# Delta rule: a chunk's decay is made one chunk ahead of its keys and queries

## The chip, the cores and the metric

The kernel runs on one core of one Trainium2 chip. The metric is device time in microseconds (us) of one execution, the median of several runs. The engines are named as in the profile: PE (TensorE matmuls; PEld its weight loads), DVE (VectorE), ACT (ScalarE), POOL (GpSimd) and SP (SyncE, which issues the DMAs; its queue is SPq).

## The reference, cut to what matters

One layer of a diffusion backbone over 2048 latent tokens and 256 context tokens, with two parallel branches. The change lies in the first one, a gated delta rule with 4 heads, run forwards and backwards. For each head and chunk of tokens it needs the decay between every two tokens of the chunk, from the running sum `G` of the log gates `g`:

```python
G = jnp.cumsum(g, axis=-1)
diff = G[..., :, None] - G[..., None, :]
decay = jnp.where(incl, jnp.exp(jnp.where(incl, diff, 0.0)), 0.0)
a_mat = jnp.where(strict, jnp.einsum('bhncd,bhnsd->bhncs', kb, k) * decay, 0.0)
...                                  # solve with (a_mat + eye)
attn = jnp.einsum('bhncd,bhnsd->bhncs', q, k) * decay
```

So the decay multiplies two products: keys with keys (for the triangular system) and keys with queries (for the attention inside a chunk). It depends on the gates alone, not on keys or queries.

## The kernel before, in words

The kernel works in chunks of 128 tokens: 18 chunks, of which 2 are context. It has these stages, in the order of the code: input norm and projection weights, the projections that give keys, queries and values (stored to DRAM as `qkvD`) and the log gates (`gD`, at about 166 us), the second branch (until about 1050 us), the chunk preparation of the delta rule (`prep`, `solve`, `levels`), the delta rule's steps (`stepA`), and the output stage.

`prep(pos)` (L732 to L806) handles one chunk. `pos` counts through `seq`: both context chunks, then the latent chunks alternately from the front and the back. In it:

- L737/L739 load keys, queries and values of the chunk into `l`, which has one buffer. PE transposes keys (`pk`, L746), queries (`pq`, L753) and values (`pv`, L764); ACT sums the squares of keys (L748) and queries (L755) and copies the transposed keys into `kv` (L749); DVE scales the values into `kv` (L765), for which it needs the norms `sk` (L756, L758) and a power that POOL takes (L757). L766 stores `kv`.
- The decay is made for each direction `d`: L773 loads the row of log gates, broadcast over the partitions, into `gb` (tag `gm`, two buffers); L777 on DVE scans it into `dc` (tag `dec`, two buffers), with a mask (`after`) that starts the sum anew at the diagonal; L779 on ACT takes the exponential; L781 on POOL zeroes the other triangle.
- L785 makes keys by keys (`pkk`), and L788 on DVE multiplies it with the decay into `an`, eight times. For latent chunks L793 makes keys by queries (`pkq`), L795 on DVE multiplies it into the decay tile in place, and L796 stores that tile to DRAM (`atN`). Blocks of `an` then go through `pk_` (L799, L801) and `dg` (L804, L805) to DRAM.

The PSUM tiles `pk`, `pq`, `pv`, `pkk` and `pkq` share one tag (`t`) with three buffers.

`solve` (L808) inverts the 32x32 diagonal blocks of four chunks at a time in a chain of small DVE operations (L821, L823). `levels` (L828) builds the larger inverse from them with small matmuls into `lvt`. In the code four `prep` calls come first, then four `levels` of the group before, then a `solve`.

After this stage the code has the gate projections (`gate_block`, L217, with the matmuls L210 to L212, weights loaded by L200 and split by L201 on ACT and L202 on POOL, results copied by L223 or L225 and stored by L226). They depend on nothing in the preparation.

The order in which each engine takes its instructions is not that of the code. When the program is built, a planner goes through it with its own estimates of durations and gives an engine that is free the earliest instruction in the code that it takes to be ready. This is how gate matmuls come between the matmuls of `prep`, and how operations of a chunk come ahead of others that stand before them in the code. The queues are fixed by then: on the chip each engine takes its instructions strictly in that order, and one that waits holds up those behind it. Buffers of a tag are given out in turn, and a write to one waits until its former content has been read.

Of the kernel before, what the change touches and what calls it, by code (L numbers as in the profile page):

```python
# [8 lines left out]
F32 = mybir.dt.float32  # L9
F32R = mybir.dt.float32r  # L10
U8 = mybir.dt.uint8
AF = mybir.ActivationFunctionType
ALU = mybir.AluOpType
# [3 lines left out]
P = 128  # L17
# [7 lines left out]
H = 4  # L25
NC = TOK // P
# [13 lines left out]
def block_kernel(ctx, tc, x, c, ctx_in, c_ctx, w_mod, b_mod, w_in, conv_w, a_log, dt_bias,  # L40
                 lb_param, a_norm_g, b_norm_g, w_a_out, w_b_out, w_out, ln_g, ln_b, out, dbg=None):
    nc = tc.nc
    sy, te, ve, ac, po = nc.sync, nc.tensor, nc.vector, nc.scalar, nc.gpsimd
# [102 lines left out]
    gD = dr.tile([2, NC, H, P], F32, name="gD")  # L146
# [342 lines left out]
    with tc.tile_pool(name="rb", reuse_waits="tile", bufs=1, side="right") as rb, \  # L489
# [12 lines left out]
        def bl(a):  # L502
            return slice(32 * a, 32 * a + 32)
# [176 lines left out]
        def gate_units(i):  # L680
            w = load_w(gcol[i])
            for g in range(NG):
                yield gate_block(i, [g], w=w)
# [3 lines left out]
        for h in range(H):  # L687
            fill = head_units(h + 1) if h + 1 < H else gate_units(NEARLY + GA)
# [24 lines left out]
    seq = list(range(NCC))  # L713
    for i in range((NC - NCC) // 2):
        seq += [NCC + i, NC - 1 - i]
    with tc.tile_pool(name="rc", reuse_waits="tile", bufs=2, side="right") as rc, \
# [7 lines left out]
        after = [rc.tile([P, H * P], U8, name=f"after{d}", bufs=1) for d in range(2)]  # L724
        for d in range(2):
            po.tensor_copy(out=after[d].rearrange("p (h t) -> p h t", h=H),
                           in_=(m_lt, m_gt)[d].bitcast(F32).unsqueeze(1).to_broadcast([P, H, P]))

        def bl(a):
            return slice(32 * a, 32 * a + 32)  # L730

        def prep(pos):  # L732
            ch = seq[pos]
            lat = ch >= NCC
            l = rc.tile([P, 3, H, P], F32, tag="l", name="l", bufs=1)
            if lat:
                sy.dma_start(out=l, in_=qkvD[ch])  # L737
            else:
                sy.dma_start(out=l[:, 0:3:2], in_=qkvD[ch, :, 0:3:2])  # L739
            kT, qT, vT = l[:, 0], l[:, 1], l[:, 2]  # L740
            kv = rc.tile([P, 2, H, P], F32, tag="kv", name="kv", bufs=1)
            sk = rc.tile([P, H], F32, tag="sk", name="sk")
            nk = rc.tile([P, H], F32, tag="nk", name="nk")
            pt = pc.tile([P, H, P], F32, tag="t", name="pk", bufs=3)
            for h in range(H):
                te.transpose(pt[:, h, :], kT[:, h, :], ident)  # L746
            for h in range(H):
                ac.activation(out=junk, in_=pt[:, h, :], func=AF.Square, accum_out=sk[:, h:h + 1])  # L748
            ac.copy(out=kv[:, 0], in_=pt)  # L749
            if lat:  # L750
                pq = pc.tile([P, H, P], F32, tag="t", name="pq", bufs=3)
                for h in range(H):
                    te.transpose(pq[:, h, :], qT[:, h, :], ident)  # L753
                for h in range(H):
                    ac.activation(out=junk, in_=pq[:, h, :], func=AF.Square, accum_out=sq[:, ch, h:h + 1])  # L755
            ve.tensor_scalar(out=sk, in0=sk, scalar1=EPS, scalar2=None, op0=ALU.add)  # L756
            po.tensor_tensor(out=nk, in0=sk, in1=half.to_broadcast([P, H]), op=ALU.pow)  # L757
            ve.reciprocal(out=sk, in_=sk)  # L758
            ve.scalar_tensor_tensor(out=nbz[:, :, ch, :], in0=beta[:, :, ch, :], scalar=-1.0,
                                    in1=sk.unsqueeze(1).to_broadcast([P, 2, H]), op0=ALU.mult, op1=ALU.mult)  # L760
            ve.tensor_tensor(out=nbze[:, :, ch, :], in0=nbz[:, :, ch, :], in1=erem[:, :, ch, :], op=ALU.mult)
            pv = pc.tile([P, H, P], F32, tag="t", name="pv", bufs=3)
            for h in range(H):
                te.transpose(pv[:, h, :], vT[:, h, :], ident)  # L764
            ve.tensor_tensor(out=kv[:, 1], in0=pv, in1=nk.unsqueeze(2).to_broadcast([P, H, P]), op=ALU.mult)  # L765
            sy.dma_start(out=knvD[ch], in_=kv)  # L766
            an = rc.tile([P, 2, H, P], F32, tag="an", name="an", bufs=1)
            dg = rc.tile([P, 2, H, 32], F32, tag="dg", name="dg", bufs=1)
            dec = []
            for d in range(2):  # L770

                gb = rc.tile([P, H * P], F32, tag="gm", name="gb")
                sy.dma_start(out=gb, in_=gD[d, ch].rearrange("h t -> (h t)").partition_broadcast(P))  # L773
                dc = rc.tile([P, H, P], F32, tag="dec", name="dec")
                dec.append(dc)
                rev = slice(None, None, -1 if d else 1)
                ve.tensor_tensor_scan(out=dc.rearrange("p h t -> p (h t)")[:, rev], data0=gb[:, rev], data1=after[d][:, rev],  # L777
                                      initial=0.0, op0=ALU.add, op1=ALU.mult)
                ac.activation(out=dc, in_=dc, func=AF.Exp)  # L779
                sgn = 1 if d == 0 else -1  # L780
                po.affine_select(out=dc, in_=dc, pattern=[[0, H], [sgn, P]], compare_op=ALU.is_ge, fill=0.0,  # L781
                                 base=0, channel_multiplier=-sgn)
            pkk = pc.tile([P, H, P], F32, tag="t", name="pkk", bufs=3)
            for h in range(H):
                te.matmul(out=pkk[:, h, :], lhsT=kT[:, h, :], rhs=kT[:, h, :], start=True, stop=True)  # L785
            for d in range(2):
                for h in range(H):
                    ve.scalar_tensor_tensor(out=an[:, d, h, :], in0=pkk[:, h, :], scalar=nbz[:, d, ch, h:h + 1],  # L788
                                            in1=dec[d][:, h, :], op0=ALU.mult, op1=ALU.mult)
            if lat:  # L790
                pkq = pc.tile([P, H, P], F32, tag="t", name="pkq", bufs=3)
                for h in range(H):
                    te.matmul(out=pkq[:, h, :], lhsT=kT[:, h, :], rhs=qT[:, h, :], start=True, stop=True)  # L793
                for d in range(2):
                    ve.tensor_tensor(out=dec[d], in0=pkq, in1=dec[d], op=ALU.mult)  # L795
                    sy.dma_start(out=atN[ch, :, d, 0], in_=dec[d])  # L796
            pk_ = rc.tile([P, H, 96], F32, tag="pk", name="pk_", bufs=1)
            for b in range(4):
                ac.copy(out=pk_[bl(b), :, 0:32], in_=an[bl(b), b % 2, :, bl(b ^ 1)])  # L799
            for d in range(2):  # L800
                ve.tensor_copy(out=pk_[64 * d:64 * d + 64, :, 32:96], in_=an[64 * d:64 * d + 64, d, :, 64 - 64 * d:128 - 64 * d])  # L801
            sy.dma_start(out=anD[ch], in_=pk_)
            for b in range(4):
                ve.transpose(out=dg[bl(b), 0].rearrange("p h j -> p (h j)"), in_=an[bl(b), 0, :, bl(b)])  # L804
                ac.copy(out=dg[bl(b), 1], in_=an[bl(b), 1, :, bl(b)])  # L805
            sy.dma_start(out=dgD[pos].rearrange("d h b i j -> (b i) (d h) j"), in_=dg.rearrange("p d h j -> p (d h) j"))  # L806

        def solve(c0, cn):  # L808

            NP = 32 * cn  # L810
            A = rc.tile([P, 32, 32], F32, tag="sA", name="sA", bufs=1)
            X = rc.tile([P, 32, 32], F32, tag="sX", name="sX", bufs=1)
            T = rc.tile([P, 256], F32, tag="sT", name="sT", bufs=1)
            Af, Xf = (t.rearrange("p i j -> p (i j)") for t in (A, X))
            sy.dma_start(out=Af[0:NP], in_=dgD[c0:c0 + cn].rearrange("c d h b i j -> (c d h b) (i j)"))
            po.memset(Xf, 0.0)
            po.memset(Xf[:, 0:1024:33], 1.0)
            for j in range(31):
                m = 31 - j
                t3 = T[0:NP, 0:m * (j + 1)].rearrange("p (i c) -> p i c", c=j + 1)  # L820
                ve.tensor_tensor(out=t3, in0=A[0:NP, j + 1:, j:j + 1].to_broadcast([NP, m, j + 1]),  # L821
                                 in1=X[0:NP, j:j + 1, 0:j + 1].to_broadcast([NP, m, j + 1]), op=ALU.mult)
                ve.tensor_tensor(out=X[0:NP, j + 1:, 0:j + 1], in0=X[0:NP, j + 1:, 0:j + 1], in1=t3, op=ALU.add)  # L823
            ac.copy(out=A[0:NP], in_=X[0:NP].rearrange("p a b -> p b a"))
            for t, i in ((Xf, 0), (Af, 1)):
                sy.dma_start(out=nD[i][c0:c0 + cn].rearrange("c d h b i j -> (c d h b) (i j)"), in_=t[0:NP])
# [93 lines left out]
    if True:  # L920
        SA = []
        for d in range(2):
            t = rd.tile([P, H, P], F32, tag=f"S{d}", name=f"S{d}")
# [78 lines left out]
        for s in range(NC):  # L1002
# [5 lines left out]
            for d in range(2):  # L1008
                ch = order[d][s]
# [205 lines left out]
```

## Time and profile before

| what | value |
|---|---|
| median of 3 runs | 2260.94 us (2259.52 to 2265.21) |
| profiled execution | 2257.96 us, its span 2256.2 us |
| mean granted PE clock | 0.981 |
| PE / DVE / ACT / POOL busy | 95% / 63% / 41% / 30% of the span |
| HBM read and written | 226.27 MB and 110.87 MB |

How to read the profile: an entry of a group gives the line of the kernel, the engine, the operation, output and inputs by name, the count, the busy time and the mean in ns of one. A wait is written as "engine tile line <- who released it: us in total, times, longest us". A wait for several things is put down to the last one. In the table by stretches each engine has its busy us and its number of instructions; the granted clock of PE is a share of full speed. PE idle is the length of a stretch less PE's busy time. Matmul records are modelled at their ends, so busy PE need not be PE at its peak.

### The profile page before, as it was taken

The numbers are of one execution on the slowest core, as the hardware profiler recorded it, in microseconds if no ns is written. First come the engines' busy times: TensorE is split into PE (matmuls) and PEld (weight loads), VectorE is DVE, ScalarE is ACT, GpSimd is POOL, SyncE is SP. The second block draws the span as 40 slices with busy tenths as digits, with TensorE's granted clock in tenths as the row PEclk, the third lists the DMA queues.
The fourth block names the chain that finished last, engine by engine and source line by source line (L and its number), as shares of the span: only waits on it lengthen the run. The fifth ranks groups of instructions, "written<-read, shape, count | busy, mean of one in ns | idle before, by whom it ended". The sixth has DMA issues, their size and how long they took to land. (4 is left out here: it accounts for less than half of the span.)

```text
span 2256.2 us, 40291 instructions
## 1 busy us (share of the span) xinstructions
PE 2135.6 (95%) x15184; PEld 1785.3 (79%) x15184; DVE 1410.5 (63%) x3235; ACT 915.4 (41%) x2314; POOL 670.5 (30%) x666
## 2 busy tenths in 40 slices
PE   7899999999999999999998898999989888999998
PEld 2778888888888888888777677778778877988887
DVE  5927666727776777785588887723332338766664
ACT  3523222224343443442555554343544345444431
POOL 2703434312221222223333332221133224433331
PEclk8999999999999999999999999999999999999999
DMA  8312222322222322225768887867888764444422
GB/s 322 96 57 66 75 65 68 84 82 79 86 83 77 111 74 87 87 72 164 234 220 241 243 241 198 251 199 227 234 267 287 254 211 160 142 140 125 141 94 80
DMA packets 303670, 339.78 MB, mean 151 GB/s; under 512 B 78123, under 2 KB 217649, under 8 KB 303475
## 3 DMA queue, kind: packets, MB, share of 16 engines
q1 hardware_dynamic: 301459, 329.87, 47.7%
q0 software_dynamic: 2016, 7.34, 0.9%
q8 instruction: 119, 1.95, 0.4%
q14 instruction: 76, 0.62, 0.1%
HBM read 226.27 MB, written 110.87 MB: 149 GB/s over the span
## 5 line engine op out<-in xcount | busy, mean ns | idle before, releaser
L210 PE MATMUL ps<-uhi,wh 128*128 128x512 f32 (+1 forms) x1824 | 707.8, 388 | 2.8 <-DVE uhi L298 2.5
L211 PE MATMUL ps<-ulo,wh 128*128 128x512 f32 (+1 forms) x1824 | 707.1, 388 | 2.8 <-DVE ulo L300 2.6
L212 PE MATMUL ps<-uhi,wl 128*128 128x512 f32 (+1 forms) x1824 | 708.0, 388 | 1.2 <-POOL wl L202 1.2
L210 PEld LDWEIGHTS ps<-uhi,wh 128*128 128x128 f32 x1824 | 346.2, 190 | 68.2 <-DVE uhi L298 3.8
L211 PEld LDWEIGHTS ps<-ulo,wh 128*128 128x128 f32 x1824 | 346.0, 190 | 66.4 <-DVE ulo L300 3.7
L212 PEld LDWEIGHTS ps<-uhi,wl 128*128 128x128 f32 x1824 | 346.1, 190 | 64.3 <-POOL wl L202 2.1
L202 POOL TENSOR_TENSOR wl<-ws,wh 128x512 fp32r<-128x512 f32 x144 | 193.3, 1342 | 582.8 <-ACT wh L201 578.9
L201 ACT CAST wh<-ws 128x512 fp32r<-128x512 f32 x144 | 89.4, 621 | 278.8 <-DMA ws<-in_w_in_dram 197.4
L398 DVE SCALAR_TENSOR_TENSOR acc<-raw,cols,acc 128x512 f32<-128x512 f32 x192 | 154.8, 860 | 0.9
L1114 PE MATMUL py<-yh,wab 128*128 128x256 f32 x512 | 145.2, 284 | 8.3 <-DVE mg L1117 6.8
L1115 PE MATMUL py<-yl,wab 128*128 128x256 f32 x512 | 144.7, 283 | 1.3 <-POOL yl L1097 1.3
L1116 PE MATMUL py<-yh,wab 128*128 128x256 f32 x512 | 144.0, 281 | 0.0
L584 POOL TENSOR_TENSOR bg<-s,fz 128x512 f32<-128x512 f32 (+1 forms) x36 | 37.5, 1041 | 259.7 <-ACT X L564 106.2
L1133 PE MATMUL pso<-uhi,mh 128*128 128x512 f32 x256 | 102.9, 403 | 8.8 <-ACT mh L1119 4.7
L1114 PEld LDWEIGHTS py<-yh,wab 128*128 128x128 f32 x512 | 97.1, 190 | 10.5 <-DVE mg L1117 8.2
L1135 PE MATMUL pso<-uhi,ml 128*128 128x512 f32 x256 | 102.2, 399 | 0.2 <-DVE ml L1120 0.2
L1134 PE MATMUL pso<-ulo,mh 128*128 128x512 f32 x256 | 101.6, 398 | 0.0
L1115 PEld LDWEIGHTS py<-yl,wab 128*128 128x128 f32 x512 | 97.3, 190 | 2.2 <-POOL yl L1097 1.7
L1116 PEld LDWEIGHTS py<-yh,wab 128*128 128x128 f32 x512 | 98.0, 191 | 0.1
L969 DVE SCALAR_TENSOR_TENSOR S<-S,gl,psA 128x128 f32<-128x128 f32 x136 | 38.3, 343 | 85.8 <-PE psA L950 85.7
L1097 POOL TENSOR_TENSOR yl<-gt,yh 128x512 fp32r<-128x512 f32 x32 | 45.5, 1424 | 147.6 <-ACT yh L1096 147.6
L401 POOL TENSOR_TENSOR acc<-acc,sg 128x512 f32<-128x512 f32 (+1 forms) x56 | 71.8, 1298 | 47.6 <-ACT sg L400 47.6
(372 smaller groups left out, 3940.4 us busy)
## 6 DMA issues: line engine op xcount, KB each, us to landing
ws<-in_w_in_dram SPq DMA_DIRECT2D x144, 256.0 KB, 3.0
gT<-gt SPq DMA_DIRECT2D x96, 256.0 KB, 3.5
kv<-knvD SPq DMA_DIRECT2D x36, 512.0 KB, 5.0
kq<-qkvD SPq DMA_DIRECT2D x32, 512.0 KB, 6.1
an<-atN SPq DMA_DIRECT2D x32, 512.0 KB, 6.3
mg<-gT SPq DMA_DIRECT2D x64, 256.0 KB, 3.4
qkvD<-acc SPq DMA_DIRECT2D x48, 256.0 KB, 2.3
l<-qkvD SPq DMA_DIRECT2D x16, 768.0 KB, 6.6
```

The costliest lines, as they stand in the source:

```text
L201: ac.copy(out=wh[:, j:j + 4, :], in_=ws)
L202: po.tensor_tensor(out=wl[:, j:j + 4, :], in0=ws, in1=wh[:, j:j + 4, :].bitcast(F32), op=ALU.subtract)
L210: te.matmul(out=ps, lhsT=wh[:, k, :], rhs=uhi[gi][:, k, :], start=(k == 0), stop=False)
L211: te.matmul(out=ps, lhsT=wh[:, k, :], rhs=ulo[gi][:, k, :], start=False, stop=False)
L212: te.matmul(out=ps, lhsT=wl[:, k, :], rhs=uhi[gi][:, k, :], start=False, stop=(k == KB - 1))
L398: ve.scalar_tensor_tensor(out=a_, in0=raw[:, o + k:o + k + n], scalar=wk, in1=a_, op0=ALU.mult, op1=ALU.add)
L1114: te.matmul(out=py[:, i, :], lhsT=wh[:, k, ms_], rhs=yh[i][:, k, :], start=(k == 0), stop=False)
L1115: te.matmul(out=py[:, i, :], lhsT=wh[:, k, ms_], rhs=yl[i][:, k, :], start=False, stop=False)
L1116: te.matmul(out=py[:, i, :], lhsT=wl[:, k, ms_], rhs=yh[i][:, k, :], start=False, stop=(k == H - 1))
L1133: te.matmul(out=ps, lhsT=mh[:, k, ts_], rhs=wout[0][k][:, ns], start=(k == 0), stop=False)
L1134: te.matmul(out=ps, lhsT=mh[:, k, ts_], rhs=wout[1][k][:, ns], start=False, stop=False)
L1135: te.matmul(out=ps, lhsT=ml[:, k, ts_], rhs=wout[0][k][:, ns], start=False, stop=(k == KB - 1))
```

## The change

The decay leaves `prep` and becomes a function `decays(pos)`. It is called for the first chunk before any `prep`, and then at the end of `prep(pos)` for the next chunk; `prep` takes the finished pair from a list. The row of log gates is loaded straight into the decay tile, and the scan works in place on it. The tag `gm` (two buffers) is gone, and the tag `dec` has four buffers instead of two, each of the same size.

```diff
+        decs = []
+
+        def decays(pos):
+
+            dec = []
+            for d in range(2):
+                dc = rc.tile([P, H, P], F32, tag="dec", name="dec", bufs=4)
+                row = dc.rearrange("p h t -> p (h t)")
+                sy.dma_start(out=row, in_=gD[d, seq[pos]].rearrange("h t -> (h t)").partition_broadcast(P))
+                rev = slice(None, None, -1 if d else 1)
+                ve.tensor_tensor_scan(out=row[:, rev], data0=row[:, rev], data1=after[d][:, rev],
+                                      initial=0.0, op0=ALU.add, op1=ALU.mult)
+                ac.activation(out=dc, in_=dc, func=AF.Exp)
+                sgn = 1 if d == 0 else -1
+                po.affine_select(out=dc, in_=dc, pattern=[[0, H], [sgn, P]], compare_op=ALU.is_ge, fill=0.0,
+                                 base=0, channel_multiplier=-sgn)
+                dec.append(dc)
+            decs.append(dec)
+
+        decays(0)
+
         def prep(pos):
...
-            dec = []
-            for d in range(2):
-
-                gb = rc.tile([P, H * P], F32, tag="gm", name="gb")
-                sy.dma_start(out=gb, in_=gD[d, ch].rearrange("h t -> (h t)").partition_broadcast(P))
-                dc = rc.tile([P, H, P], F32, tag="dec", name="dec")
-                dec.append(dc)
-                rev = slice(None, None, -1 if d else 1)
-                ve.tensor_tensor_scan(out=dc.rearrange("p h t -> p (h t)")[:, rev], data0=gb[:, rev], data1=after[d][:, rev],
-                                      initial=0.0, op0=ALU.add, op1=ALU.mult)
-                ac.activation(out=dc, in_=dc, func=AF.Exp)
-                sgn = 1 if d == 0 else -1
-                po.affine_select(out=dc, in_=dc, pattern=[[0, H], [sgn, P]], compare_op=ALU.is_ge, fill=0.0,
-                                 base=0, channel_multiplier=-sgn)
+            dec = decs.pop(0)
...
             sy.dma_start(out=dgD[pos].rearrange("d h b i j -> (b i) (d h) j"), in_=dg.rearrange("p d h j -> p (d h) j"))
+            if pos + 1 < NC:
+                decays(pos + 1)
```

## The prediction

> **What bounds the kernel now.** I read the page's busy times first, then the stages, then who waited for whom in the stage that the change touches, then one chunk in order of time.
>
> ```profile
> span 2256.2 us, 40291 instructions
> PE 2135.6 (95%) x15184; PEld 1785.3 (79%) x15184; DVE 1410.5 (63%) x3235; ACT 915.4 (41%) x2314; POOL 670.5 (30%) x666
> ```
>
> TensorE (PE) is busy for 95% of the span, so the matmuls set the time, and a change that removes no matmul can win only what PE idles or runs slowly: 2256.2 - 2135.6 = 120.6 us in all. Where that lies is in the table by stage (columns: stretch, length, busy us of PE, PEld, DVE, ACT, POOL, granted PE clock, DMA share, GB/s). The chunk preparation runs from about 1052 to 1398 us.
>
> ```profile
> 1050.00:1100.00 50.00, 48.38 (x250) 40.78 (x249) 28.78 (x71) 23.93 (x77) 21.93 (x25) 1.00 0.80 241
> 1100.00:1400.00 300.00, 265.34 (x1941) 214.94 (x1940) 247.19 (x649) 153.47 (x523) 95.25 (x114) 0.96 0.78 233
> 1400.00:1640.00 240.00, 228.81 (x2335) 189.69 (x2335) 105.36 (x323) 102.26 (x317) 44.78 (x70) 0.99 0.74 222
> 1640.00:1830.00 190.00, 171.42 (x1145) 153.69 (x1145) 57.57 (x173) 78.99 (x259) 55.60 (x44) 0.96 0.79 256
> ```
>
> From 1050 to 1400 PE idles 1.6 + 34.7 = 36.3 us; from 1100 to 1400 its clock is 0.96, worth another 0.04 x 300 = 12 us. So the stage loses some 48 us, and DVE, busy 247.19 / 300 = 82%, is the second busiest engine there. Gate matmuls, which depend on nothing in this stage, fill PE between the chunk's own; they are placed in PE's queue beforehand, so a chunk matmul that is late stops those behind it too. PE's waits from 1040 to 1420 us:
>
> ```profile
> PE pkk L785 <- ACT kv L749: 10.5, 10, 1.8
> PE pk L746 <- DMA l<-qkvD: 6.4, 6, 1.6
> PE pkq L793 <- ACT junk L755: 5.0, 6, 1.9
> PE pkq L793 <- DVE kv L765: 3.7, 4, 2.4
> PE lvt L871 <- DVE yt L868: 3.5, 4, 1.5
> PE lvt L853 <- DVE yt L849: 2.3, 2, 2.1
> PE lvt L859 <- DVE N L856: 2.1, 2, 1.3
> ```
>
> The largest are waits for a PSUM buffer: the five tiles pk, pq, pv, pkk and pkq share three buffers, and pkk needs ACT to have copied pk out (L749), pkq needs ACT's squares of pq (L755) or DVE's product (L765). Why is ACT late? The waits of all engines in the same stretch, and SP's own:
>
> ```profile
> ACT dec L779 <- DVE dec L777: 60.6, 30, 4.5
> DVE dec L777 <- DMA atN<-dec: 19.1, 10, 4.1
> SPq L773 <- DVE dec L777: 19.9, 15, 3.1
> ```
>
> ACT stands 60.6 us, 30 times, in front of the decay's exponential, and part of that is DVE standing in front of the scan until the previous chunk's attention tile has been stored out of the same two buffers. One chunk shows the chain:
>
> ```profile
> 1210.65 1.22 DVE L777 TENSOR_TENSOR_SCAN dec<-gb,after 128x512 f32<-128x512 f32 x1
> ...
> 1211.90 0.63 ACT L779 ACTIVATE dec<-dec 128x512 f32<-128x512 f32 x1 [1.66 <-DVE dec L777]
> ...
> 1214.41 0.58 ACT L749 COPY kv<-pk 128x512 f32<-128x512 f32 x1
> ...
> 1215.04 1.96 PE L785 MATMUL pkk<-l 128*128 128x128 f32 x8 [1.53 <-ACT kv L749]
> 1215.97 0.63 ACT L779 ACTIVATE dec<-dec 128x512 f32<-128x512 f32 x1 [0.99 <-DVE dec L777]
> ...
> 1218.39 2.05 PE L793 MATMUL pkq<-l 128*128 128x128 f32 x8 [0.54 <-DVE kv L765]
> ```
>
> Although the code has the scans behind L765, the planner has put each exponential in ACT's queue ahead of the squares and the copy of its own chunk. ACT waits 1.66 us for the scan, then does squares and copy, and PE waits 1.53 us for the copy. Without the exponential in that place (1.66 + 0.63 us) the copy would not have been late.
>
> **The change part by part.** Per chunk the step issues two loads, two scans, two exponentials and two selects; no count changes over the 18 chunks. Prices:
>
> ```profile
> L777 DVE TENSOR_TENSOR_SCAN dec<-gb,after 128x512 f32<-128x512 f32 x36 | 47.3, 1317 | 28.8 <-DMA atN<-dec 19.1 <-issue 6.8 <-DMA gb<-gD 1.7
> L781 POOL TENSOR_SCALAR_AFFINE_SELECT dec<-dec 128x512 f32<-128x512 f32 x36 | 28.3, 788 | 59.5 <-ACT dec L779 54.8 <-DMA ws<-in_w_in_dram 2.7 <-issue 2.0
> L779 ACT ACTIVATE dec<-dec 128x512 f32<-128x512 f32 x36 | 22.6, 632 | 60.7 <-DVE dec L777 60.6
> l<-qkvD SPq DMA_DIRECT2D x16, 768.0 KB, 6.6
> gb<-gD SPq DMA_DIRECT2D x36, 256.0 KB, 4.2
> atN<-dec SPq DMA_DIRECT2D x32, 256.0 KB, 3.3
> ```
>
> Busy time. Scans 47.3, selects 28.3 and exponentials 22.6 us stay as they are: in place or not, the scan reads and writes as many elements. The two row tiles and two decay tiles of before become four tiles of the same size, so SBUF space is equal. 0 us.
>
> ACT's waits in front of the copy and the squares. The exponential of the next chunk no longer needs this chunk's buffers (four tiles are two chunks), so its rows, scan and exponential can be done in gaps of the chunk before. The two PE waits on ACT add to 10.5 + 5.0 = 15.5 us. Bounds: all of it goes (-15.5), or none, because the squares also wait for the load of l (0). ACT's 60.6 us in front of the exponential are four times PE's 15.5, so most of it can be laid to them; I take two thirds: -10.
>
> DVE's product (L765), behind the second scan in the same chunk. PE waits 3.7 us for it. Bounds -3.7 and, if the next chunk's scans now stand in front of it, +2 x 1.317 us on each of 18 chunks = +47 us of DVE delay (a rival below). I take -2, half, since the reciprocal in front of L765 also waits for a POOL power.
>
> The waits of the level matmuls (lvt, 3.5 + 2.3 + 2.1 = 7.9 us) are on DVE and could gain where DVE stood in front of a scan (19.1 us in 10 places), or lose as much where a scan is put before the copies. Between -4 and +4; taken 0.
>
> SP. The row load waited 19.9 us on SP for the scan that frees its buffer, with weight loads, gate stores and the chunk's stores behind it. It will wait for a store of two chunks earlier instead, which lands in 3.3 us and was issued a chunk ago, so that wait should be empty. What of this reaches PE is the gate weights, and none of the large PE waits is on them: 0, between -1 and, if the planner sets the load too early in the queue, one 3.3 us landing on a few chunks (+5). The moved loads pass the load of l, the stores of the chunk and the weight loads on SP; the selects (0.788 us) pass the power and the weight subtraction on POOL, 95.25 / 300 = 32% busy: 0.
>
> What is late next: the load of l. It has one buffer, is issued when pkq's matmuls are through, and takes 6.6 us.
>
> ```profile
> L737 SPq DMA_DIRECT2D l<-qkvD x16: 319/430/932, 1073.2 to 1363.4; - x16
> ```
>
> Chunks follow each other every (1363.4 - 1073.2) / 15 = 19.3 us. DVE work per chunk is 0.82 x 19.3 = 15.9 us, so preparation can speed up by 3.4 us a chunk at most; each such speed-up leaves less filler under the 6.6 us, and PE's 6.4 us on this load grow. Between 0 and +10 (6 times 1.6, the longest seen); taken +3. A shorter stage itself wins nothing, since the filler that it does not use comes later, and nearly all of it finds PE free to take it.
>
> The first chunk's decay, now ahead of everything, takes 4.2 + 1.3 + 0.6 + 0.8 us under filler matmuls, and if this cover were gone it would cost those 7 us once. 0.
>
> The clock. Stalls in a cluster cost twice:
>
> ```profile
> 1210.00:1215.00 5.00, 3.09 (x27) 2.22 (x25) 4.87 (x10) 3.23 (x12) 1.95 (x2) 1.00 0.88 264
> 1215.00:1220.00 5.00, 4.42 (x17) 3.73 (x18) 4.95 (x16) 2.61 (x11) 1.70 (x2) 0.52 0.65 161
> ```
>
> After 5 us with PE 3.09 us busy the next 5 us are granted 0.52 of the clock. A third of the stage's 12 us, in step with about a third of its stalls: -4 (bounds 0 and -12).
>
> The Trainium skill, "TensorE: Matmul & The Clock Gate", section "What's actually happening", ties the throttling to an idle window of some 3.4 us. By that rule gaps of 0.5 to 2 us would cost no clock, the term would be 0 and the sum 4 us smaller in gain; the rows above show the clock halved after such shorter gaps, so here the measurement stands against the rule read narrowly.
>
> **Sum:** -10 - 2 + 3 - 4 = -13 us. The profiled execution took 2257.96 us (span 2256.2 and 1.8 around it), 2.98 below the median of 2260.94; so 2244.96 for such an execution and 2260.94 - 13 = 2248 for the median.
>
> **The rivals.**
> No change that can be measured. The stalls move from ACT to the load of l, or the planner sets the scans and exponentials where they were. For it: l's load is in the same cycle, and PE already has filler; the atN wait is only 19.1 us on DVE, in 10 of 36 scans. Against it: PE's largest wait names ACT, not the load. With l at its +10 and the clock unmoved: -10 - 2 + 10 = -2, so 2259.
>
> Slower: the next chunk's scans stand in front of this chunk's work on DVE. DVE is at 82%, and a scan that is ready early, with its exponential, can be placed ahead of L765 or of the products with pkk, which free the PSUM buffers that PE waits for. Price: 47 us of DVE delay as worked out above; of such waits now, 19.1 + 60.6 us, PE sees 15.5 + 3.7, a quarter; the other engines' slack and the filler cover the rest. A quarter to a half of 47 is +12 to +24, which eats the gain: 18 chunks x 0.7 us of PE stall = 13 us is the point from which it decides. At +24 with the ACT gain of 10 kept: 2275. Against it: the scan already waits there today, in front of the same chunk's work.
>
> A larger gain. All PE waits on ACT and on L765 go (15.5 + 3.7), with the clock's 12: -31, 2230. Against it: l's load, and the level matmuls, which keep breaking the stream.
>
> **How the numbers follow.** My forecast (some 6 to 20 us less) 0.42; the larger gain 0.13; no change 0.24; slower 0.21, since every engine's order in the following stages is drawn up anew as well, which the 11.2 and 18.6 us of PE idle from 1400 to 1830 leave room for in both directions. The likeliest time is 2248, its own range 2240 to 2255. To leave no more than 2 in 10 outside, the range goes from 2229 (the larger gain) to 2272 (most of the slower case). About 0.3%, 6.8 us, is what a measurement can tell from no change: faster 0.55, same 0.24, slower 0.21.
>
> **What would show it.** Right: ACT's wait in front of the exponential falls far below 60.6 us; the scan no longer waits for the store of dec; PE's waits at L785 and L793 on ACT halve; PE idle between the first and last chunk falls by about 9 us, and the granted clock rises above 0.96; the wait on l grows. Wrong: PE's waits for L765 or for pk on l exceed what left ACT; or the loss appears after 1400 us, in the delta steps, with the preparation itself faster.

## The result and the profile after

The changed kernel takes 2287.38 us (median of 4 runs, 2284.77 to 2288.51), the kernel before 2262.78 (4 runs, 2259.52 to 2265.21): ratio 1.012, 95% interval 1.0099 to 1.0142. The forecast was 2248 in a range from 2229 to 2272; the change costs some 25 us, with the sign opposite to the forecast.

First the page after and the same four stretches as before (columns: stretch, length, busy us of PE, PEld, DVE, ACT, POOL, granted clock, DMA share, GB/s):

```profile
span 2283.1 us, 40287 instructions
PE 2146.6 (94%) x15184; PEld 1794.7 (79%) x15184; DVE 1412.3 (62%) x3235; ACT 914.4 (40%) x2314; POOL 671.4 (29%) x666
```

```profile
1050.00:1100.00 50.00, 45.97 (x230) 37.78 (x229) 32.07 (x71) 22.08 (x71) 22.60 (x26) 1.00 0.68 210
1100.00:1400.00 300.00, 259.69 (x1836) 210.78 (x1835) 227.21 (x593) 147.60 (x508) 89.27 (x110) 0.94 0.74 225
1400.00:1640.00 240.00, 228.35 (x2230) 189.47 (x2229) 116.81 (x354) 98.62 (x305) 43.71 (x63) 0.97 0.73 218
1640.00:1830.00 190.00, 167.40 (x1243) 150.06 (x1241) 61.07 (x184) 81.70 (x264) 55.41 (x50) 0.92 0.78 258
```

The number of matmuls is the same, and PE idles more in each stretch: 4.0 + 40.3 us up to 1400 where it was 1.6 + 34.7, at a clock of 0.94 instead of 0.96, and the clock is lower in the two later stretches too. DVE does less in 1100 to 1400 (227.21 us, was 247.19): the preparation runs late, it is not overloaded.

Stretches of fixed ends cut the work of the two kernels at different points. A better cut is the last gate matmul that can fill PE before the levels end (to 1 us, 1610 before and 1636 after), and the next gate matmul (1662 and 1689). First the kernel before, then the changed one:

```profile
1050.00:1610.00 560.00, 518.10 (x4128) 424.11 (x4128) 366.61 (x993) 261.15 (x854) 155.99 (x194) 0.98 0.76 227
1610.00:1662.00 52.00, 41.09 (x590) 35.99 (x587) 23.22 (x75) 30.91 (x108) 10.99 (x18) 0.97 0.88 270
```

```profile
1050.00:1636.00 586.00, 530.13 (x4223) 434.73 (x4222) 374.51 (x1011) 265.28 (x872) 154.31 (x198) 0.96 0.73 221
1636.00:1689.00 53.00, 40.72 (x480) 36.16 (x479) 18.59 (x57) 23.03 (x80) 9.81 (x14) 0.74 0.66 206
```

At the end of the second row both have done the same matmuls (4718 and 4703 records), the changed kernel 27 us later, which is the whole difference of the spans (2283.1 - 2256.2 = 26.9). Idle PE makes 15.3 of it (55.87 + 12.28 after, 41.90 + 10.91 before), longer busy time for the same matmuls, at a lower clock, the other 11.7.

Who waits for whom from 1040 to 1420 us, PE first, then DVE, ACT and SP's queue (us in total, times, longest):

```profile
PE pkq L801 <- DVE kv L786: 16.0, 9, 3.6
PE pkq L801 <- ACT junk L776: 14.9, 6, 4.4
PE pkk L793 <- ACT kv L770: 8.1, 6, 2.1
PE pk L767 <- DMA l<-qkvD: 2.5, 3, 1.6
```

```profile
DVE dec L742 <- DMA dec<-gD: 50.2, 18, 9.4
ACT dec L744 <- DVE dec L742: 63.0, 25, 7.1
SPq L740 <- DMA atN<-dec: 14.2, 13, 2.5
```

The scan's wait for its row was 1.7 us; it is 50.2. SP now waits for the attention tile's store in 13 places, and PE's waits for `pkq` have grown from 8.7 to 30.9 us. By groups (busy us, mean ns, then idle time in front), the scan itself got no dearer:

```profile
L742 DVE TENSOR_TENSOR_SCAN dec<-dec,after 128x512 f32<-128x512 f32 x36 | 44.9, 1252 | 53.8 <-DMA dec<-gD 50.2 <-issue 3.2 <-POOL sX L826 0.3
```

One chunk of the changed kernel in order of time (start, us, engine, line):

```profile
1209.88 0.50 SPq L804 DMA_DIRECT2D atN<-dec  x1
...
1210.94 0.81 SPq L804 DMA_DIRECT2D atN<-dec  x1
...
1213.38 0.46 SPq L740 DMA_DIRECT2D dec<-gD  x1
...
1218.44 1.22 DVE L742 TENSOR_TENSOR_SCAN dec<-dec,after 128x512 f32<-128x512 f32 x1 [7.54 <-DMA dec<-gD]
...
1219.70 0.63 ACT L744 ACTIVATE dec<-dec 128x512 f32<-128x512 f32 x1 [3.03 <-DVE dec L742]
...
1220.23 0.26 ACT L776 ACTIVATE junk<-pq 128x128 bf16<-128x128 f32 x1
...
1221.04 2.08 PE L801 MATMUL pkq<-l 128*128 128x128 f32 x8 [3.83 <-ACT junk L776]
1221.06 0.69 DVE L786 TENSOR_TENSOR kv<-pv,nk 128x512 f32<-128x512 f32 x1
```

The attention tiles of one chunk are stored at 1209.88 and 1210.94. The row for the chunk two further on goes into the same tile, so its load is issued 3.5 us after the store, at 1213.38. The scan of that row stands in DVE's queue in front of the next chunk's product L786, and so DVE stands for 7.54 us. ACT, whose queue has the exponential in front of the last two squares, stands for 3.03 us, and PE's `pkq` for 3.83 us. "Four tiles are two chunks" was right, and the planner used both: in the queues of the changed kernel the decays run two chunks ahead of the attention tiles' stores, so that the store in front of the load is again the one just issued, and behind it comes a load that in the kernel before was done a chunk early, into a row tile of its own.

The order of work on DVE has changed less than this may sound. In both traces two scans stand between one chunk's last attention product (L795 before, L803 after) and the next chunk's product with `pv` (L765 and L786); only in four chunks of the changed kernel one of the two comes behind it, and its last chunk has none left in front. Before, they were that chunk's own scans, with their rows nearly always landed; after, they are the scans of the chunk behind it, with rows that are often still under way.

### The profile page after: what moved, and what is told of

It reads as the page before. It is cut to its first block, busy times and chain, and to the rows that moved or that the text cites. A ratio compares the mean times of both kernels' runs of the same rounds, so it can differ in the third digit from the quotient of the medians.

```text
span 2283.1 us, 40287 instructions
## 1 busy us (share of the span) xinstructions
PE 2146.6 (94%) x15184; PEld 1794.7 (79%) x15184; DVE 1412.3 (62%) x3235; ACT 914.4 (40%) x2314; POOL 671.4 (29%) x666
## 5 line engine op out<-in xcount | busy, mean ns | idle before, releaser
L1107 POOL TENSOR_TENSOR yl<-gt,yh 128x512 fp32r<-128x512 f32 x32 | 44.9, 1407 | 149.5 <-ACT yh L1106 149.5
L1117 ACT ACTIVATE mg<-mg 128x512 f32<-128x512 f32 x64 | 40.4, 632 | 112.3 <-DMA mg<-gT 108.0
```

## The experiments

The main theory: the row of log gates lands late, because its tile is the decay's own, and DVE's and ACT's queues stand behind it. Against it stand these rivals: the place of the next chunk's scans and exponentials, in front of this chunk's work, costs by itself (the prediction's slower rival); the traffic of the loads costs; each redrawn order has a price of its own; the exponential's place on ACT costs. A letter in an expectation means what that expectation says with it.

### The move alone, and the shared tile alone

`decays()` is called a chunk ahead as in the change, but with the two row tiles and two decay tiles of before:

```diff
-dc = rc.tile([P, H, P], F32, tag="dec", name="dec", bufs=4)
-sy.dma_start(out=row, in_=gD[d, seq[pos]]...)
+dc = rc.tile([P, H, P], F32, tag="dec", name="dec")
+gb = rc.tile([P, H * P], F32, tag="gm", name="gb")
+sy.dma_start(out=gb, in_=gD[d, seq[pos]]...)
```

> Move alone: decays(pos + 1) is called at the end of prep(pos) as in the changed kernel, but with the buffers of before, two row tiles and two decay tiles, and the scan not in place. Theory A (the loss comes from the row being loaded into the decay tile: the load has to wait for the store of the attention out of that tile, and the scan then stands on DVE for it): as before, 2255 to 2270. Rival B (the move itself, the next chunk's scan in front of this chunk's work, costs the time): as the changed kernel, 2280 to 2290.

Measured: 2263.68 us, ratio 1.0019 (0.9998 to 1.0041), no difference clear of noise. On DVE the scans of a chunk stand where they stood before. The place in the code has little say: the planner issues what it takes to be ready, and two decay tiles are ready no earlier wherever the call is written.

The other half, the kernel before with the row loaded into one of four decay tiles, where the code has it:

```diff
-gb = rc.tile([P, H * P], F32, tag="gm", name="gb")
+dc = rc.tile([P, H, P], F32, tag="dec", name="dec", bufs=4)
+gb = dc.rearrange("p h t -> p (h t)")
```

> In place with four tiles, not moved: the decay stays where it stood in prep. Theory A: as slow as the changed kernel, 2278 to 2292, with some 50 us of DVE waits for the row. Rival B: as before, 2255 to 2270.

Measured: 2269.76 us, ratio 1.0044 (1.0025 to 1.0063). The wait for the row appears without the move, and in the trace the next chunk's scans stand ahead of the product as in the changed kernel:

```profile
DVE dec L777 <- DMA dec<-gD: 37.1, 19, 9.9
```

So the sharing brings it, but with 37.1 us and 10 us of time it is less than was expected; sharing and move together have 13 us more of this wait and 0.8% more time.

### Between them: one row tile, three decay tiles

```diff
+dc = rc.tile([P, H, P], F32, tag="dec", name="dec", bufs=3)
+gb = rc.tile([P, H * P], F32, tag="gm", name="gb", bufs=1)
```

> Moved ahead as in the change, but the four tiles are split as one row tile and three decay tiles, the scan not in place. Theory A: the row no longer waits for the store of the attention, only for the scan before it, so no long wait of DVE for the row as in the changed kernel; a second row load comes close before its scan, some 10 to 20 us of wait: 2255 to 2270. Rival B2 (any look ahead of more than two decay tiles costs the time): 2275 to 2290.

Measured: 2271.73 us, ratio 1.0062 (1.0042 to 1.0082), just above what was expected, and with a longer wait for the row than the 10 to 20 us expected. With one row tile, the second direction's load has to wait for the first one's scan:

```profile
DVE dec L743 <- DMA gb<-gD: 32.1, 13, 5.6
```

Four decay tiles beside row tiles of their own, the version that would have both, were not tried.

### No row, half the rows, rows twice

The scan of the changed kernel over a constant column, without the loads:

```diff
-sy.dma_start(out=row, in_=gD[d, seq[pos]]...)
-ve.tensor_tensor_scan(out=row[:, rev], data0=row[:, rev], data1=after[d][:, rev],
+ve.tensor_tensor_scan(out=row[:, rev], data0=nhalf.to_broadcast([P, H * P]), data1=after[d][:, rev],
```

> The changed kernel without the row loads: the scan reads a constant column, broadcast, in place of the log gates, so the decay is not the gates' one. Nothing else is left out. Theory A: the wait in front of the scan goes, 2240 to 2260. Rival D (the place of the scans, in front of this chunk's product L786 on DVE, costs the time even with the row there): 2270 to 2290.

Measured: 2256.76 us, ratio 0.9996 (0.9978 to 1.0014). The whole loss is gone, although the scans stand ahead of the products as in the changed kernel and ACT waits as long as there:

```profile
ACT dec L743 <- DVE dec L741: 63.1, 32, 6.4
DVE dec L741 <- DMA atN<-dec: 25.6, 10, 6.5
```

The rival of the place on DVE falls: by itself it costs nothing here, and 63.1 us of ACT waiting cost nothing either. ACT's order is another one, though. In the trace of the changed kernel 17 of the 36 exponentials stand behind the first square of a chunk's queries and ahead of its copies into `dg`; here 3 do, and none in the kernel before. Since this run takes away the traffic too, the kernel before was run with each row loaded twice:

```diff
 sy.dma_start(out=gb, in_=gD[d, ch]...)
+sy.dma_start(out=gb, in_=gD[d, ch]...)
```

> The kernel before with each row of log gates loaded twice into its own tile, 36 more loads of 256 KB. Tells whether e5_no_row_load was fast because the loads' traffic was gone. Theory A (their lateness, not their traffic): within 0.4% of before, 2250 to 2268. Rival E (traffic or SP issue time): 10 us or more slower, 2270 to 2285.

Measured: 2262.49 us, ratio 1.0018 (1.0002 to 1.0034). Twice the loads of rows that land early cost some 4 us, 8 at most, of some 25: traffic isn't the main cause. And the changed kernel with the rows of every second chunk only:

```diff
-sy.dma_start(out=row, in_=gD[d, seq[pos]]...)
+if pos % 2 == 0:
+    sy.dma_start(out=row, in_=gD[d, seq[pos]]...)
```

> The changed kernel with the row of log gates loaded for every second chunk only; the scans of the other chunks run over a constant column instead, so nine of the eighteen decays are made of other numbers than the reference's. The scans, exponentials and selects keep their count, and on DVE the next chunk's scans stand ahead of this chunk's product as in the changed kernel. Theory A (what costs is DVE standing for a row that is loaded late into the shared tile): about half of it is left, DVE waits 20 to 30 us for the row instead of 50.2 from 1040 to 1420 us, and the kernel is 8 to 18 us slower than before (ratio 1.003 to 1.008). Rival B (each redrawn order of the later stages has a price of its own, whatever the rows do): no place in the middle is to be expected; the time is as without loads (within 0.3%) or as with all of them (1.010 to 1.014).

Measured: 2276.87 us, ratio 1.007 (1.0048 to 1.0091), in the middle, as a cost in step with the late rows would be. The wait for the row has halved and more:

```profile
DVE dec L743 <- DMA dec<-gD: 19.1, 8, 9.8
DVE dec L743 <- DMA atN<-dec: 12.5, 9, 5.8
```

This is weaker than it looks. With the waits of the scans that have no row, DVE idles 31.8 us in front of its scans, 3 us more than the 28.8 of the kernel before. And a time in the middle doesn't exclude a price of the redrawn order: other kernels with redrawn orders, above and below, lie in the middle too.

### Giving the load, the scan, or both their old room

All four kernels here leave the tiles of the changed kernel and only bind the order. First the scan and the exponential, behind this chunk's last work on DVE and ACT (`vi`, `ai`: the last transpose and copy into `dg`):

```diff
-decays(pos + 1)
+decays(pos + 1, (vi.ins, ai.ins))
...
+with ExitStack() as order:
+    for i in behind:
+        order.enter_context(tc.issue_after(i))
+    ve.tensor_tensor_scan(...)
+    ac.activation(out=dc, in_=dc, func=AF.Exp)
```

> The changed kernel, with the scans and exponentials of the next chunk bound to stand behind the last DVE and ACT work of this chunk's preparation. The row then has a chunk's time to land. Theory A: the wait for the row falls below 10 us and the time to that of before or below, 2245 to 2265. Rival C (what the changed kernel loses is another drawing of the later stages, not this wait): 2275 to 2290 although the wait is gone.

Measured: 2269.67 us, ratio 1.0048 (1.0028 to 1.0067): a miss, some of the loss stays. DVE's wait for the row is gone, but the load still stands early on SP, now 30.7 us in front of the store, with the chunk's other transfers behind it:

```profile
SPq L740 <- DMA atN<-dec: 30.7, 18, 4.4
PE pk L770 <- DMA l<-qkvD: 9.7, 5, 6.1
```

That these two waits are what still costs is not shown. PE waits longer for `l` in kernels that take the time of before (16.3 us with the rows twice, 13.2 with both bound, below), and with the rows twice SP stands 24.6 us in front of a row load without harm. The cut at the gate matmuls says the same: PE reaches the last one 3 us later than in the kernel before (4128 matmuls by 1610 us), with 40 matmuls more done. The loss lies behind it, and the clock there is 0.77 (0.97 before):

```profile
1050.00:1613.00 563.00, 520.87 (x4168) 427.27 (x4166) 368.47 (x1004) 266.62 (x866) 154.95 (x193) 0.97 0.77 229
1613.00:1666.00 53.00, 39.58 (x529) 34.93 (x524) 18.47 (x63) 24.36 (x83) 11.03 (x18) 0.77 0.68 206
```

Then the load alone, behind this chunk's store of `kv` (L787; `li` is that store):

```diff
-decays(pos + 1)
+decays(pos + 1, (li.ins,))
...
+with ExitStack() as order0:
+    for i in after_load:
+        order0.enter_context(tc.issue_after(i))
+    sy.dma_start(out=row, in_=gD[d, seq[pos]]...)
```

> The changed kernel with one edit: the row loads for the next chunk are bound to stand on SP behind this chunk's knvD store. The store of the attention that they wait for is then a chunk old. Theory A (late rows and the SP queue standing for the store): DVE's wait for the row and SP's wait for the store both fall below 10 us, time 2250 to 2264. Rival C (another drawing of the order, whatever it is, costs 10 us or more): 2268 to 2285 with both waits gone.

Measured: 2276.14 us, ratio 1.0093 (1.0067 to 1.0119): the largest miss. DVE's wait is down to

```profile
DVE dec L745 <- DMA dec<-gD: 21.5, 10, 5.3
```

and yet three quarters of the loss remain, but in another place. The same cut at the last gate matmul, of this kernel:

```profile
1050.00:1615.00 565.00, 520.31 (x4100) 427.14 (x4099) 366.16 (x996) 265.23 (x859) 154.54 (x194) 0.97 0.75 225
1615.00:1681.00 66.00, 45.65 (x601) 40.88 (x601) 21.26 (x68) 26.50 (x92) 10.91 (x18) 0.77 0.66 198
```

It reaches the last gate matmul 5 us later than the kernel before, with 28 matmuls fewer done. The 52 us after that, in which level and step matmuls run without filler, take it 66 us, at 20.4 us of idle PE (10.9 before) and a clock of 0.77 (0.97). What makes this stretch longer was not isolated; the two kernels that follow have as many matmuls there, some 600, and take 60 us. DVE idles 21.9 us in front of the scans of this kernel, less than the 28.8 before. So the rival of another order, which foresaw this time (though with both waits gone), is not out.

Both bindings together, and then both without the exponential's on ACT:

```diff
+decays(pos + 1, (vi.ins, ai.ins), (li.ins,))   # both
+decays(pos + 1, (vi.ins,), (li.ins,))          # the exponential left free
```

> As the run before, and in addition the scans and exponentials are bound behind this chunk's last DVE and ACT work, as in e4_scan_behind. Theory A: e4 was 11 us slower than before because SP stood 30.7 us for the store in front of the load of l and others; with that gone 2248 to 2262. Rival C: 2266 to 2280, as e4, because the steps behind the preparation stay long.

Measured: 2261.13 us, ratio 1.0014 (0.9997 to 1.003). The changed tiles with the load and the scan at their old distance take the time of before.

> The changed kernel with the row loads bound behind this chunk's store of kv on SP and the scans bound behind this chunk's last transpose on DVE, but the exponentials left free on ACT. Theory A (the place on DVE and SP matters, ACT only follows the scan): as with both engines bound, ratio 0.999 to 1.004, DVE waits under 10 us for the row. Rival C (the exponential's place on ACT, ahead of this chunk's squares and copies, is what cost 0.9% with the load alone bound): 1.006 to 1.011, with the waits of PE on ACT's squares and copies (pkq and pkk) above 20 us together from 1040 to 1420 us.

Measured: 2259.72 us, ratio 1.001 (0.9992 to 1.0028), so with DVE and SP bound, ACT needs no binding. It does not test the rival of the place on ACT: in both traces the exponentials stand in the same places among the squares and copies, none of them behind a square of queries as in the changed kernel. The row's wait, first with both and then with the exponential free:

```profile
DVE dec L748 <- DMA dec<-gD: 5.8, 6, 1.7
```

```profile
DVE dec L748 <- DMA dec<-gD: 5.5, 6, 2.1
```

### All together

The waits and counts are those of one profiled execution each, which can lie off the median: both bound 2270.45 us (median 2261.13), load bound 2282.09 (2276.14), half the rows 2282.48 (2276.87).

| kernel | ratio | DVE's wait for the row, us | level matmuls left after 1640 us |
|---|---|---|---|
| before | 1 | 1.7 | 80 |
| no row loads | 0.9996 | none | 112 |
| both bound, exponential free | 1.001 | 5.5 | 128 |
| both bound | 1.0014 | 5.8 | 128 |
| rows twice (before) | 1.0018 | 6.9 | 128 |
| move alone | 1.0019 | 0.8 | 88 |
| shared tile alone | 1.0044 | 37.1 | 192 |
| scan bound | 1.0048 | gone; SP 30.7 for the store | 136 |
| one row tile | 1.0062 | 32.1 | 224 |
| half the rows | 1.007 | 19.1 | 224 |
| load bound | 1.0093 | 21.5 | 240 |
| changed | 1.012 | 50.2 | 256 |

Every kernel in which neither DVE waits long for the row nor SP for the store in front of its load stays within 0.2% of before, and every kernel with such a wait is at least 0.4% slower.

Shown: the row's load into the shared tile, without a chunk's distance to its scan, is the cause of the changed kernel's loss. Sharing the tile costs without the move, the move costs nothing clear of noise without the sharing, and the loss goes when the loads are left out and when load and scan get back their distance. The loads' traffic is at most a smaller part of it, and the scans' place on DVE by itself costs nothing.

Not shown: the way from the late row to the lost time. The size doesn't follow the wait for the row among the slow ones (21.5 us at 1.0093, 37.1 at 1.0044). Nor does it follow all idle time of DVE in front of the scans, whoever ended it: 28.8 us before and 53.8 in the changed kernel, but 35.1 with the rows twice, 21.9 with the load bound and 1.3 with the scan bound. The planner draws up the queues anew for each kernel, and how much of the loss comes with those orders, ACT's among them, stays open.

The last column follows the ratio almost without exception, with the scan bound the odd one. It is a measure of how late the levels are, not proof of a cause. Nor is it just the preparation ending late. Its last store (`dgD`) is issued at 1397 us before and at 1411 us in the changed kernel, but at 1407 without row loads and at 1413 with the rows twice, both at no loss to speak of, and at 1402 with the load bound, which is 0.9% slower.

## Why the prediction was wrong, step by step

- **What bounds it** held: only PE's idle time and clock moved. Busy PE counts 2146.6 instead of 2135.6 us for the same 15184 matmuls.
- **The step that failed is the one on SP**, "that wait should be empty", priced between -1 and +5. It assumed that two chunks' worth of tiles leave the planner one chunk ahead. The planner took all that the buffers allow, two chunks, and the wait is 14.2 us in 13 places. Worse, the step ended at the store. Behind it comes the load, and in a shared tile the scan can't have its row before both. The row of the forecast's own quotation, 1.7 us on `gb`, was the one at risk: a separate row tile was the reason for that small number. In its place stand 50.2 us.
- **ACT's waits, -10.** "Falls far below 60.6 us" did not come: 63.0. PE's waits on ACT went from 15.5 to 23.0 us. And the premise was weak: without row loads ACT waits 63.1 us at no loss, so this wait didn't measure what there was to win.
- **DVE's product, -2** with bounds to the other side: PE's wait for it went from 3.7 to 16.0 us. The upper bound's condition came true (the next scans stand in front of it).
- **The slower rival** named the right place and the right sign, and its 2275 is 12 us short. Its price was wrong in kind: 18 x 2 scans' busy time. That is not added, since two scans, the chunk's own, stood in that place before, as the rival's "against it" says; without row loads the place costs nothing (0.9996). What comes with the loss is a scan standing there for a row.
- **The load of l, +3**: the reverse. It lands sooner, and PE's wait fell from 6.4 to 2.5 us. The moved DMAs in the stretch of the chunks (KB, median us from issue to landing):

```profile
l<-qkvD SPq DMA_DIRECT2D x16, 768.0 KB, 5.2
dec<-gD SPq DMA_DIRECT2D x36, 256.0 KB, 4.7
```

- **The clock, -4**: the sign failed with the stalls'. Of the 27 us some 12 are matmuls at a lower clock. They are not in step with the stalls, as the term assumed: the lowest clock, 0.74, is that of the last 53 us, where idle PE grew only from 10.9 to 12.3 us.
- **Busy time, 0**: held (scan 1252 ns, was 1317). Level matmuls in the chunk stage, "between -4 and +4": their waits of 7.9 us there nearly vanished, but after 1411 us the wait of `lvt` for `yt` (L878 after, L868 before) grew from 2.1 to 9.6.
- **Signs named as proof.** "PE's waits for L765 ... exceed what left ACT" was the one that told; "the preparation itself faster" did not come, since the loss begins within it.

## What to carry to other kernels

A prefetch has a distance, and it lives in a buffer that nothing else holds: folding the landing tile into the result tile keeps the bytes equal, and here, with four such tiles, it took that distance away until the places of load and scan were bound. Where a planner fills every free buffer, more tiles mean work issued further ahead, again up against the store that frees them; ask of each load which read or store frees its tile, and what stands behind its consumer in an in-order queue. Price a moved step by the waits it can bring along, not by its busy time, and don't take a wait for something to win until it is seen that the engines behind it are late for it.

## What the hardware showed that was not expected

PE's busy share doesn't tell its clock. In the stretch between the gate matmuls PE was busy for 77% of the time in the changed kernel and 79% in the one before (40.72 of 53 and 41.09 of 52 us, rows above), and the granted clock was 0.74 against 0.97. What decides between the two was not tried.

The load into the decay tile took 4.7 us from issue to landing, a little longer than the row's 4.2 us before. With the 3.5 us between the issues of store and load in the chunk shown, that is 8 us in which a tile is neither decay nor row, about two fifths of the 19.3 us of a chunk. The Trainium skill, "DMA: Bandwidth & Descriptors", section "Rules for kernel authors", says to issue a DMA early and wait for it late; the runs agree, 1.0014 with the distance given back against 1.012 without it.
